# Expert units take their token rows by gathers from a normalized copy in DRAM instead of one-hot products

## The chip, the cores and the metric

The kernel runs on one core of a Trainium2 chip. The metric is the device time of one execution in microseconds (us). TensorE (PE) does the matmuls, VectorE (DVE), ScalarE (ACT) and GpSimd (POOL) the rest; SyncE (SP), ACT and POOL start transfers between DRAM and the on-chip memory, which 16 DMA engines carry out.

## The reference

512 tokens of width 1024 pass two layers of a first block and one of a second block. The change lies in the last stage, a mixture of experts with 32 experts in 4 groups, of which every token uses two:

```python
def hierarchical_moe(xn, w_group, b_group, w_expert, b_expert, w_gate, w_up, w_down):
    ...
    top_val, top_idx = lax.top_k(e_in, EXPERT_TOP_K)
    weights = p_group[:, None] * jax.nn.softmax(top_val, axis=-1)
    ...
    def run_block(args):
        tok, wt, e = args
        xb = xt[tok]
        hmid = jax.nn.silu(xb @ w_gate[e]) * (xb @ w_up[e])
        return (hmid @ w_down[e]) * wt[:, None].astype(xb.dtype)
    ...
# h = h + hierarchical_moe(rms_norm_2(h, g_ffn), ...), then rms_norm_2(h, g_final)
```

`xt` are the 512 normalized rows, `xb` those of the tokens that chose expert `e`. Everything is float32.

## The kernel before

Nearly all of the program before the experts is the same in both kernels. Each tile of 128 tokens keeps its rows in `h[t]` on the chip. As a tile gets ready, `moe_logits` (L1118) turns its rows, multiplies them with the gate weights and works out `r`, the factor that normalizes each row (`rstd`); `rn` keeps it. `moe_route` finds each token's two experts and the rank of each pick in its expert. `moe_first` (L1213) makes the tables of the first four blocks, `moe_plan` (L1229) those of all the others (`key`, `si`), on VectorE.

The picks of an expert fill blocks of 64 slots. A *unit* is one block with one expert's weights. There are 35 units: 32 first blocks, and at the units 8, 15 and 22 a second block of the same expert (here 8b, 15b, 22b), which uses weights that are already there. The first four units (`EARLY`) have fixed experts; which expert the others work for comes from `moe_plan`, and SP loads its number into a register before it starts their weights.

Each expert's weights are three pieces of 2 MiB: two for the way up (`gu`), one for the way down (`y`). They come by SP's queue into nine slots, so three experts' worth is on the chip; a piece for unit p+3 is started when the piece of unit p in its slot has been used for the last time, and SP starts the pieces one after the other, so that one that must wait holds up those behind it.

The loop in `moe` (L1459) writes, for unit u: `upwards` (the products `gu` with two of the pieces, then tanh on ACT and two products on DVE, tile `th`), `taken(u + 1)` (the next unit's rows), `down` (the products `y` of unit u-1, a copy, and a scatter of its rows to `picked` in DRAM by POOL), `hidden` (two transposes of `th`, tile `hT`), `turned` (four transposes of the next unit's rows `xg`, scaled by DVE into `xT`). The build may move instructions of different steps past each other where the data allow it.

`taken` (L1364) makes, on DVE, a one-hot matrix from the keys (tiles `kb`, `o`, `oh`), scaled with `rn`, multiplies it with all 512 rows on the tensor engine, and copies the result to `xg` on ACT:

```python
        for t in range(NT):
            for h in range(2):
                self.mm(pt[64 * h : 64 * h + 64, :], oh[:, t, :], self.h[t][:, 512 * h : 512 * h + 512],
                        start=t == 0, stop=t == NT - 1, tile_position=(0, 64 * h))
        nc.scalar.copy(xg, pt)
```

The products of one expert's work and these share the line L123 or L113 of the helpers `tr` and `mm`; in the profile they are told apart by tiles: `tr<-h,oh` are the one-hot products, `tr<-kf,xg` and `tr<-kf,th` the transposes, `gu<-we,xT` and `y<-we,hT` the expert's products. L1359 starts the weights, L1434 the scatters. After the loop the last unit's rows are weighed on the chip, `finish` (L1520) reads the scattered rows back, adds them, normalizes and writes the result.

Of the kernel before, what the change touches and what calls it, by code (L numbers as in the profile page):

```python
# [11 lines left out]
F32 = mybir.dt.float32  # L12
I32 = mybir.dt.int32
U32 = mybir.dt.uint32
AF = mybir.ActivationFunctionType
ALU = mybir.AluOpType
AX = mybir.AxisListType
PSUM = bass.MemoryType.PSUM
DRAM = bass.MemoryType.DRAM

P = 128
D = 1024
S = 512
# [3 lines left out]
EARLY = 4  # units whose experts are fixed  # L27
SECOND = (8, 15, 22)  # units whose experts may have a second block
NB = 32 + len(SECOND) + 16  # blocks of picks
HALF = (1, 0) * 32  # which of a token's weighted rows the tensor engine sums  # L30
# [36 lines left out]
class Beside:  # L67
    """A stage of n steps that runs beside others, from start to end on their scale."""
# [22 lines left out]
class K:  # L91
    """State that the stages of the kernel share."""
# [22 lines left out]
    # issue inst only once other is done, so that the group inst belongs to stays together  # L115
# [9 lines left out]
    # ---------------------------------------------------------------- set-up  # L125
# [34 lines left out]
    # (scale * x + eps) ** -0.5 for a narrow x: first guess from the bits, then Newton steps  # L160
# [19 lines left out]
    # dst[:, k, :] = transpose(h * rstd) * gs (+ sh), gs and sh per channel  # L180
# [14 lines left out]
    def psum_phase(self, **psbufs):  # L195
        """The PSUM rings of the phase that starts here."""
        es = ExitStack()
        self.ps = self.pool("ps", space=PSUM, es=es, reuse_waits="tile")
        self.psbufs = psbufs
        return es  # L200
# [5 lines left out]
    # where the experts' rows go, by picks; rows are read before the last have come  # L206
    def picked_open(self):
        self.yd = self.nc.dram_tensor("picked", [2 * S + NB, D], F32, kind="Internal").ap()
        self.yv = dram_disjoint_views(self.yd, 4)  # no two blocks scatter to the same row
        z = self.gp.tile([P, 2 * D], F32, tag="g", name="g")  # L210
        self.nc.gpsimd.memset(z, 0.0)
        for n in range(4):
            self.nc.gpsimd.dma_start(self.yd[n * 256 : n * 256 + 256, :].rearrange("(p r) d -> p (r d)", r=2), z)
# [9 lines left out]
    # ------------------------------------------------------- adaLN vectors  # L223
# [16 lines left out]
    # vector j (of 14, 1024 wide) of silu(c) @ [ada_w[0] | ada_w[1] | kv_ada_w] + bias: the products of  # L240
    # each partition are summed on the vector engine, or each of four groups of columns of the tensor
    # engine sums those of a fourth of the chunks; the sum over the partitions follows
# [52 lines left out]
    # g * (1 + scale) per channel  # L295
# [10 lines left out]
    # a row that comes by itself into t, early; later it is spread over the partitions by a product with ones  # L306
# [11 lines left out]
    # ------------------------------------------------------------- HGRN2  # L318
# [25 lines left out]
    # Within a tile of 128 tokens the decays are taken relative to the bounds of blocks of 16, 32, 64  # L344
    # and 128, so that no exponent but that of the 16-token blocks' own keys is positive.
    def hgrn(self, tiles, gs, sh, bufs, whole=False):
# [26 lines left out]
        for hd in range(8):  # L373
# [48 lines left out]
            # keys and queries relative to the bounds inside the tile  # L422
# [23 lines left out]
            # and relative to the tile's bounds  # L446
# [79 lines left out]
    # -------------------------------------------------------------- PEER  # L526
# [32 lines left out]
    # what goes into the PEER layer, by rows  # L559
# [8 lines left out]
    # expert numbers and gates of the tiles' 64 picks per token; alone: of each tile by itself  # L568
# [52 lines left out]
    # expert numbers and gates of a head's 16 picks, from the scores of its two halves  # L621
    def pick(self, sc):
# [39 lines left out]
        # exp(x) = ((1 + tanh(x / 4)) / (1 - tanh(x / 4))) ** 2: tanh lies in one table with gelu  # L662
# [62 lines left out]
    # ---------------------------------------------- stick-breaking mixer  # L725
# [4 lines left out]
    def sb(self, tiles, gk, shk, gq, shq):  # L730
# [50 lines left out]
        lo = [max(n - t0, 0) * P for n in range(nk)]  # first query column that key block n serves  # L781
        at = [(n % 2) * 256 for n in range(nk)]  # where block n lies in its bank
# [57 lines left out]
    # ------------------------------------- second block up to its experts  # L840
# [25 lines left out]
    # room for these tiles; early: their gates are worked out beside the attention  # L866
# [39 lines left out]
    # the first block's last norm  # L906
# [6 lines left out]
    # convolution and attention of some of the tiles  # L913
    def b2_first(self, tiles):
# [61 lines left out]
        # weights that are still there are used first  # L976
# [81 lines left out]
    # what follows on them, for all the tiles  # L1058
# [26 lines left out]
    # the way out  # L1085
# [13 lines left out]
    # ------------------------------------------------------------ experts  # L1099
    def moe_setup(self):  # L1100
# [8 lines left out]
        self.si0 = mp.tile([P, EARLY], I32, name="si0")  # L1109
        self.perm = mp.tile([P, 32], I32, name="perm")  # L1110
# [6 lines left out]
    # logits of tile t (of a pair), from its rows and what normalizes them  # L1117
    def moe_logits(self, t, space):  # L1118
# [15 lines left out]
        nc.vector.tensor_copy(self.rn[:, t : t + 1], r)  # L1134
        nc.vector.scalar_tensor_tensor(self.lg[:, t % 2, :], pl[:, :36], r, self.bge, op0=ALU.mult, op1=ALU.add)

    # experts, weights and ranks of the picks of tiles t and t + 1
    def moe_route(self, t):
# [47 lines left out]
        # weights: group probability times softmax over the two  # L1186
# [9 lines left out]
    # rows to gather (two halves of each token's row) and rows to scatter to for n blocks of 64 slots, from the  # L1196
    # slots and the blocks (one-hot) of the picks
    def moe_table(self, tag, n, slot, blocks, si):
# [10 lines left out]
        # an empty block's first slot takes a row that is there, and leaves one that no one reads  # L1209
        V.tensor_tensor(out=si, in0=f, in1=self.caps[:, :n], op=ALU.min)  # L1210

    # the tables of the first units' blocks, which need no more than the ranks
# [11 lines left out]
    # Experts are numbered from the last one down. Each one's picks fill blocks of 64 slots. Unit p works  # L1224
    # off the first block of one expert: of expert p, but that the first experts from EARLY on with more
    # than 64 picks change places with others, so that they lie at the units SECOND; their second blocks
    # follow there. Whatever else there is goes to further blocks, of which at most 16 are filled.
    # For each pick: its block and slot; for each block: the rows to scatter to.
    def moe_plan(self):  # L1229
# [26 lines left out]
        # least e whose prefix sum exceeds j, for j = 0 .. n - 1  # L1256
# [23 lines left out]
        # which expert each unit works for, and where each expert lies  # L1280
# [3 lines left out]
        for j, p in enumerate(SECOND):  # L1284
# [6 lines left out]
            # without such an expert, qe is zero and nothing moves  # L1291
# [12 lines left out]
        # block and slot of each pick  # L1304
# [30 lines left out]
        self.moe_table("y", NB, slot, av, self.si)  # L1335
        em = locate(ing, 16, "lm")
# [8 lines left out]
    def moe_open2(self):  # L1345
# [4 lines left out]
        self.xg = [self.mx.tile([P, 512], F32, name=f"xg{j}") for j in range(2)]  # L1350
        self.ng = 0

    # the weights of unit n, of expert e, by pieces: two that go up, and one that goes down
# [8 lines left out]
    # The rows of a block's tokens, those whose key in blocks lies from block on: a product of all  # L1362
    # rows with a one-hot matrix takes them.
# [19 lines left out]

    def space(self):
        self.ng += 1
        return self.xg[self.ng % 2]
# [12 lines left out]
    # Both halves of the tensor engine's columns work at a time: first each on half of the hidden  # L1399
    # units, then each on half of the outputs, for the same 64 tokens.  # L1400
# [38 lines left out]
    # where in a block a token's row goes, by weight: for either half of the outputs, slots by tokens  # L1439
# [19 lines left out]
    def moe(self):  # L1459
# [3 lines left out]
        units = []  # weights and block  # L1463
# [5 lines left out]
        def taken(u):  # L1469
            b = units[u][1]  # L1470
            return self.taken(self.key0, 64.0 * b) if b < EARLY else self.taken(self.key, float(b))
# [5 lines left out]
        x = self.turned(taken(0))  # L1477
        self.moe_plan()
        late = []
        last = len(units) - 1  # L1480
        for u, (p, b) in enumerate(units):
# [5 lines left out]
            x = taken(u + 1)  # L1487
# [3 lines left out]
            x = self.turned(x)  # L1491
            late.append((p, b, hT))
        down()
        # the last unit's rows are added on the chip
# [6 lines left out]
        # blocks that are left: then all over again, with all rows from DRAM  # L1501
# [13 lines left out]
    # an expert's number, for the engine that loads its weights  # L1515
# [3 lines left out]
    # the rows of the picks, by weight, from DRAM and from y, and the last norm  # L1519
# [41 lines left out]
    # ------------------------------------------------------------- program  # L1561
# [137 lines left out]
FIN = (0, 1, 1, 1)  # how many of a tile's two rows the tensor engine weighs at the end  # L1699
# [18 lines left out]
def prep(i):  # L1718
    """The inputs laid out for the kernel."""
# [3 lines left out]
    def kmaj(w, n):  # [K, N] -> [N / n, 128, K / 128, n]  # L1723
        k, m = w.shape
        return lay(w.reshape(k // P, P, m // n, n).transpose(2, 1, 0, 3))
# [13 lines left out]
    q, f, v, g = (w[:, o : o + 1024].reshape(8, P, 8, P) for o in (0, 1024, 2048, 3072))  # k p h n  # L1739
# [55 lines left out]
```

## Time and profile before

| | |
|---|---|
| times of three runs | 2838.49, 2839.49, 2849.84 us; median 2839.49 us |
| the profiled execution, first to last instruction | 2837.1 us (its own whole time is not given; the median lies 2.4 us above its span) |
| busy: PE, DVE, ACT, POOL | 86%, 69%, 28%, 26% of the span |
| DMA over the whole span | 342 GB/s |
| the loop over units | from about 2260 us to 2797 us of the span, then the last unit and the end |

Busy shares are means over stages that have different limits. What a change in the loop over units can be worth is read in that loop.

### The profile page before, as it was taken

To read this page: it belongs to the slowest core of one execution; us is meant where nothing else is said; L and a number is where in the kernel's file an instruction comes from. 1 tells how busy PE (TensorE), PEld (TensorE's weight loads), DVE (VectorE), ACT (ScalarE), POOL (GpSimd) and SP (SyncE) were. 2 spreads that over 40 slices of the span, in tenths; PEclk is the share of its full clock that TensorE was granted. 3 is DMA by queue.
4 is the path that set the end of the run, shared out by engine and by line. 5 is a ranking of instruction groups with operands and counts; after the bars stand their busy time and mean duration, and the time that the engine had idled before them with its cause. 6 is when DMAs were issued, how large, how long until landed. Compare 5 with 4: busy or idle time off the path is not lost.

```text
span 2837.1 us, 31101 instructions
## 1 busy us (share of the span) xinstructions
PE 2446.9 (86%) x10210; PEld 1491.1 (53%) x10210; DVE 1967.1 (69%) x5490; ACT 808.2 (28%) x1918; POOL 731.2 (26%) x576
## 2 busy tenths in 40 slices
PE   5999888878798787599887769689999999999997
PEld 3786456645466454166564435256888633333332
DVE  3886899997996689965577999878777532222224
ACT  2542255562221812122661121333113000000001
POOL 0000233333334344443343435423420000000000
PEclk9999989998999798799999879799999999999999
DMA  9875889999899799899889979888998679889794
GB/s 406 324 271 195 315 328 366 385 355 380 339 400 416 288 394 373 325 405 374 315 327 371 368 290 369 329 322 310 412 384 312 234 310 412 322 347 400 310 416 179
DMA packets 121556, 970.22 MB, mean 342 GB/s; under 512 B 15268, under 2 KB 16676, under 8 KB 20528
## 3 DMA queue, kind: packets, MB, share of 16 engines
q0 software_dynamic: 79904, 587.06, 53.3%
q1 hardware_dynamic: 39280, 375.51, 32.9%
q10 hardware_dynamic: 2208, 5.63, 0.6%
q8 instruction: 82, 1.34, 0.2%
q14 instruction: 82, 0.67, 0.1%
HBM read 955.71 MB, written 17.33 MB: 343 GB/s over the span
## 4 chain that ended last, share of the span: by engine, by line
PE 51%; DVE 27%; DMA 9%; issue 6%; ACT 6%; POOL 1%; ACTq 0%; POOLq 0%; SPq 0%; DVEq 0%
PE pj L113 16%; PE gu L113 9%; DVE g L697 8%; PE acc L113 7%; DMA g<-in_uv_dram,ex 6%; PE y L113 5%; PE tr L113 4%; PE rt L113 4%; PE mm L113 4%; DVE acc L716 4%; DVE y L947 3%; PE ad L113 2%; POOL g L694 1%; DMA w<-in_hgw_dram 1%; PE tr L123 1%
## 5 line engine op out<-in xcount | busy, mean ns | idle before, releaser
L694 POOL DMA_INDIRECT g<-in_uv_dram,ex x512 | 682.4, 1333 | 1173.8 <-DVE acc L716 431.9
L113 PE MATMUL acc<-g,dg 128*128 128x512 f32 x1056 | 595.0, 697 | 194.2 <-ACT dg L708 193.8
L697 DVE SCALAR_TENSOR_TENSOR g<-g,hn 128x1024 f32<-128x1024 f32 x512 | 621.4, 1218 | 102.1 <-DMA g<-in_uv_dram,ex 98.3
L113 PEld LDWEIGHTS acc<-g,dg 128*128 128x128 f32 x1056 | 215.6, 217 | 445.3 <-ACT dg L708 264.0
L716 DVE SCALAR_TENSOR_TENSOR acc<-g,wt,acc 128x1024 f32<-128x1024 f32 x240 | 306.7, 1278 | 3.5
L113 PE MATMUL gu<-we,xT 128*64 128x512 f32 x1120 | 256.6, 593 | 0.8 <-DVE xT L1394 0.8
L113 PE MATMUL pj<-hT,w 128*128 128x256 f32 (+1 forms) x1136 | 215.6, 344 | 4.4 <-DMA w<-in_win_dram 2.9
L1434 POOL DMA_INDIRECT picked<-y,si x34 | 33.2, 977 | 676.6 <-DVE y L1430 459.4
L113 PEld LDWEIGHTS pj<-hT,w 128*128 128x128 f32 x1136 | 185.6, 193 | 39.5 <-issue 16.5
L113 PE MATMUL pj<-hTa,w 128*128 128x256 f32 x768 | 180.9, 381 | 0.9 <-DVE sg L408 0.9
L113 PE MATMUL pj<-w,hT 128*128 128x256 f32 (+1 forms) x832 | 177.7, 371 | 0.0
L701 ACT ACTIVATE wt<-hid 128x2 f32<-128x2 f32 x256 | 51.8, 203 | 424.6 <-DVE g L697 423.3
L113 PEld LDWEIGHTS pj<-w,hT 128*128 128x128 f32 x832 | 152.7, 190 | 26.7 <-issue 8.1
L113 PEld LDWEIGHTS gu<-we,xT 128*64 128x64 f32 x1120 | 81.9, 137 | 159.6 <-issue 145.9
L1413 DVE SCALAR_TENSOR_TENSOR th<-th,gu 128x256 f32<-128x256 f32 x35 | 14.7, 421 | 214.9 <-ACT th L1412 214.9
L113 PEld LDWEIGHTS pj<-hTa,w 128*128 128x128 f32 x768 | 141.0, 191 | 24.4 <-issue 5.6
L113 PE MATMUL tr<-h,oh 128*64 128x512 f32 x560 | 152.7, 602 | 0.0
L113 PE MATMUL y<-we,hT 128*64 128x512 f32 x560 | 148.8, 593 | 0.2
L113 PE MATMUL rt<-hn2T,w 128*128 128x256 f32 (+1 forms) x640 | 123.7, 341 | 1.8 <-ACT hn2T L585 1.8
L708 ACT ACTIVATE dg<-kf,wt 128x128 f32<-128x128 f32 x264 | 101.5, 397 | 80.8 <-DVE wt L702 72.6
L947 DVE SCALAR_TENSOR_TENSOR y<-vb,wdw,y 128x128 f32<-128x128 f32 (+1 forms) x360 | 121.2, 389 | 1.4 <-ACT y L943 0.6
L113 PEld LDWEIGHTS rt<-hn2T,w 128*128 128x128 f32 x640 | 102.3, 193 | 23.0 <-issue 11.2
(476 smaller groups left out, 3366.0 us busy)
## 6 DMA issues: line engine op xcount, KB each, us to landing
we<-in_we_dram SPq DMA_DIRECT2D x96, 2048.0 KB
aw<-in_adaw_dram POOLq DMA_DIRECT2D x20, 2048.0 KB, 9.4
w<-in_win_dram SPq DMA_DIRECT2D x34, 1024.0 KB
w<-in_hgw_dram SPq DMA_DIRECT2D x32, 1024.0 KB
w<-in_pwq_dram SPq DMA_DIRECT2D x16, 1024.0 KB
w<-in_kvw_dram SPq DMA_DIRECT2D x16, 1024.0 KB
aw<-in_adaw_dram SPq DMA_DIRECT2D x4, 2048.0 KB
w<-in_hgwo_dram SPq DMA_DIRECT2D x8, 1024.0 KB
```

The source lines that it names most:

```text
L113: return self.nc.tensor.matmul(out, lhsT, rhs, start=start, stop=stop, **kw)
L123: return self.nc.tensor.transpose(out, in_, self.ident[:n, :n])
L694: nc.gpsimd.indirect_dma_start(out=g, out_offset=None, in_=uv, in_offset=bass.IndirectOffsetOnAxis(ap=picks[r // 16][0][:, r % 16 : r % 16 ...
L697: nc.vector.scalar_tensor_tensor(g[:, 0:D], g[:, 0:D], 1.0, hn, op0=ALU.mult, op1=ALU.mult, accum_out=hid[:, r : r + 1])
L701: nc.scalar.activation(wt[:, bs], hid[:, bs], AF.Gelu)
L708: nc.scalar.activation(dg, self.ident, AF.Copy, scale=wr)
L716: nc.vector.scalar_tensor_tensor(acc, g[:, D:], wr, acc, op0=ALU.mult, op1=ALU.add)
L947: nc.vector.scalar_tensor_tensor(y[:, c, :], vb[:, c, j : j + T], self.wdw[:, c, j : j + 1], y[:, c, :], op0=ALU.mult, op1=ALU.add)
L1413: nc.vector.scalar_tensor_tensor(th, th, 1.0, pg[:, :256], op0=ALU.add, op1=ALU.mult)
L1434: self.nc.gpsimd.indirect_dma_start(out=yv.rearrange("v (h d) -> (v h) d", h=2), out_offset=bass.IndirectOffsetOnAxis(ap=si, axis=0), in_= ...
```

## The change

For every unit from the fifth on (u = 4 to 34) the one-hot product goes. `moe_logits` now also writes the normalized rows of its tile to a DRAM tensor `xd` (one more pass of ACT over the tile and one transfer of 512 KB from ACT's queue). `moe_plan` works out a table `gi` of the rows to gather (four more small operations on DVE). `gathered` starts an indirect transfer on POOL's queue that fetches up to 128 half rows of 2 KB, those of one block, into `xg`. There are three `xg` now, and the loop asks for the rows of unit u+2 while it works on unit u. The first four units keep the one-hot products. The diff also takes out all comments; that is not shown.

```diff
 def moe_setup:
+        self.gi = mp.tile([P, NB], I32, name="gi")
+        self.xd = self.dp.tile([S, D], F32, name="xd")
 def moe_logits:
         nc.vector.tensor_copy(self.rn[:, t : t + 1], r)
+        xn = xT[:, 1].rearrange("p k n -> p (k n)")
+        nc.scalar.activation(xn, self.h[t], AF.Copy, scale=r)
+        nc.scalar.dma_start(self.xd[t * P : (t + 1) * P, :], xn)
 def moe_plan:
         self.moe_table("y", NB, slot, av, self.si)
+        odd = ts(tl(NB, "vi", I32), self.si, 1, None, ALU.bitwise_and)
+        ts(self.gi, self.si, 2, 1, ALU.logical_shift_right, ALU.logical_shift_left)
+        tt(self.gi, self.gi, odd, ALU.add)
+        ts(self.gi, self.gi, self.capg, None, ALU.min)
 def moe_open2:
-        self.xg = [self.mx.tile([P, 512], F32, name=f"xg{j}") for j in range(2)]
+        self.xg = [self.mx.tile([P, 512], F32, name=f"xg{j}") for j in range(3)]
+    def gathered(self, b):
+        xg = self.space()
+        self.nc.gpsimd.indirect_dma_start(
+            out=xg, out_offset=None, in_=self.xd.rearrange("s (h d) -> (s h) d", h=2),
+            in_offset=bass.IndirectOffsetOnAxis(ap=self.gi[:, b : b + 1], axis=0),
+            bounds_check=2 * S - 1, oob_is_err=False)
+        return xg
     def space(self):
         self.ng += 1
-        return self.xg[self.ng % 2]
+        return self.xg[self.ng % 3]
 def moe:
-        def taken(u):
-            b = units[u][1]
-            return self.taken(self.key0, 64.0 * b) if b < EARLY else self.taken(self.key, float(b))
+        rows = {}
+        def take(u):
+            if u <= last and u not in rows:
+                b = units[u][1]
+                rows[u] = self.taken(self.key0, 64.0 * b) if b < EARLY else self.gathered(b)
...
             th = self.upwards(p, x)
-            x = taken(u + 1)
+            take(u + 1)
+            if units[min(u + 2, last)][1] >= EARLY:
+                take(u + 2)
             if late:
                 down()
             hT = self.hidden(th)
-            x = self.turned(x)
+            x = self.turned(rows.pop(u + 1))
```

## Rows read from the trace of the kernel before

**Rows 1.** The page: span, and busy time of each engine (share) xinstructions.
```profile
span 2837.1 us, 31101 instructions
PE 2446.9 (86%) x10210; PEld 1491.1 (53%) x10210; DVE 1967.1 (69%) x5490; ACT 808.2 (28%) x1918; POOL 731.2 (26%) x576
```

**Rows 2.** Chain that ended last, 2399 to 2432 us: start, length, work.
```profile
2406.93 2.58 PE tr L113 x12
2410.36 3.43 PE y L113 x14
2413.79 0.81 PE tr L123 x6
2414.60 1.00 PE tr L113 x2
2415.60 6.87 PE gu L113 x31
```

**Rows 3.** Waits of PE, 2306 to 2797 us: total, times, longest.
```profile
PE tr L123 <- DVE th L1414: 16.9, 12, 1.5
```

**Rows 4.** Stretches: length, busy time by engine (xinstructions), granted clock, DMA share, GB/s.
```profile
2306.80:2783.00 476.20, 460.80 (x2127) 161.84 (x2124) 114.41 (x237) 42.02 (x94) 30.15 (x31) 1.00 0.90 369
2306.00:2417.50 111.50, 111.50 (x502) 37.05 (x502) 27.47 (x57) 9.46 (x21) 7.81 (x8) 1.00 0.98 401
2417.50:2430.00 12.50, 12.50 (x60) 4.24 (x56) 3.10 (x7) 1.17 (x3) 0.00 (x0) 1.00 0.01 5
2592.00:2652.00 60.00, 54.07 (x258) 19.63 (x257) 13.76 (x28) 4.82 (x11) 3.88 (x4) 1.00 1.01 427
2668.00:2682.00 14.00, 14.00 (x67) 4.74 (x64) 3.16 (x8) 1.35 (x3) 0.00 (x0) 1.00 0.06 18
2718.00:2768.00 50.00, 45.55 (x219) 16.62 (x217) 10.61 (x22) 4.05 (x9) 2.91 (x3) 1.00 1.01 428
2784.00:2797.00 13.00, 11.42 (x58) 4.04 (x56) 4.28 (x12) 0.77 (x2) 1.07 (x1) 1.00 0.03 12
```

**Rows 5.** Waits of SP's queue, 2399 to 2433 us: total, times, longest.
```profile
SPq L1359 <- PE tr L123: 22.2, 1, 22.2
```

**Rows 6.** DMA queues and issues, 2258 to 2837 us: packets, MB, share; KB each.
```profile
q1 hardware_dynamic: 13680, 188.75, 79.3%
q0 software_dynamic: 2720, 4.02, 1.9%
...
we<-in_we_dram SPq DMA_DIRECT2D x87, 2048.0 KB
```

**Rows 7.** Groups by line, 2306 to 2797 us: busy us, mean ns, idle before.
```profile
L113 PE MATMUL tr<-h,oh 128*64 128x512 f32 x496 | 133.7, 597 | 0.0
...
L1394 DVE TENSOR_TENSOR xT<-tr,cv 128x512 f32<-128x512 f32 x32 | 22.1, 692 | 14.0 <-PE tr L123 11.8
```

**Rows 8.** Chain that ended last, 2600 to 2617 us.
```profile
2602.23 3.58 PE tr L113 x16
```

**Rows 9.** One line's instructions (L1434, the scatters): ns min/median/max, landing.
```profile
L1434 POOL DMA_INDIRECT picked<-y,si x34: 966/971/1067, 2291.0 to 2798.1; - x34
...
DMA to landing us min/median/max: 2.5/8.1/10.2
```

**Rows 10.** Timeline of ACT and DVE ahead of the loop: start, length, instruction.
```profile
2238.24 1.06 ACT L176 ACTIVATE tmp<-h 128x1024 f32<-128x1024 f32 x1
...
2249.86 0.16 DVE L1369 TENSOR_SCALAR kb<-key 128x8 f32<-128x8 f32 x1
```

**Rows 11.** Chain that ended last, 2270 to 2840 us: units 3 and 31.
```profile
2306.80 6.87 PE gu L113 x31
...
2797.11 6.87 PE gu L113 x32
```

**Rows 12.** Stretches ahead of the loop, columns as in rows 4.
```profile
2241.80:2245.80 4.00, 1.31 (x6) 1.04 (x5) 3.79 (x33) 0.41 (x2) 0.00 (x0) 0.50 0.96 376
2245.80:2252.50 6.70, 6.69 (x30) 6.57 (x30) 4.56 (x21) 0.00 (x0) 0.00 (x0) 0.50 1.03 429
```

More of the change, by code (lines that the diff above doesn't have):

```diff
@@ L1475, in down @@
             self.scatter(self.downwards(n, hT), self.si0[:, b : b + 1] if b < EARLY else si[:, b : b + 1], self.yv[b % 4])
-        x = self.turned(taken(0))
+        last = len(units) - 1
+        take(0)
+        x = self.turned(rows.pop(0))
         self.moe_plan()
         late = []
-        last = len(units) - 1
         for u, (p, b) in enumerate(units):
```

## The prediction

> **What bounds the kernel now.** The page comes first: PE is busy for 86% of the span [rows 1]. That is a mean over stages, so the next view is the chain of waits inside the loop over units. There it runs over PE alone: one step, from the first `gu` of a unit to that of the next, is 15.54 us: 6.87 for `gu`, then the one-hot products, 3.43 and a little more for `y`, the transposes, and 1.00 in which two of the next unit's one-hot products stand between the transposes and the next `gu` [rows 2]. The waits of PE say the same: in 490 us it waits 16.9 us for `th` and for nothing else, never for weights [rows 3]. So at first sight whatever is taken from PE is gained.
>
> The stretches show what stands right behind PE. From the start of unit 3 to 2783 us, when the last weights have come, the DMA engines are busy for 0.90 of the time and move 369 GB/s [rows 4]. That mean hides two kinds of time. Over 111.5 us without a hole the share is 0.98, and at two later places 1.01. The rest is three holes of 12.5 to 14.0 us (two are shown) in which next to nothing moves [rows 4]. They lie at the second blocks, which need no weights: SP waits 22.2 us in one go for the slot that the late `y` of a unit frees [rows 5]. Outside the holes the weights are almost as slow as PE: a transfer-bound step lies just under a PE-bound one.
>
> **What the change removes from PE.** 31 units lose 16 one-hot products each; the group has 496 [rows 7]. Where they stand in one piece on the chain they take 3.58 us [rows 8]. Where the order is that of rows 2, two of them cover the time in which DVE makes `xT` (692 ns) [rows 7]; then up to 1.00 us [rows 2] comes back as idle time, if the build puts nothing else there. So a step loses between 2.58 and 3.58 us and becomes 12.0 to 13.0 us. For PE alone, 31 steps give 80 to 111 us: a span of 2726 to 2757 us. The removed work on DVE and ACT lies beside PE, so it counts for nothing.
>
> **What the weights allow.** The stretch from 2306.8 to 2783 us moved 369 GB/s x 476.2 us = 175.7 MB [rows 4]. The gathers add about what the scatters move, the same picks the other way: 4.02 MB for 34 of them [rows 6], so 3.7 MB for 31. Together 179.4 MB. The rate is the term that decides. Its lower bound is 401 GB/s (the first stretch, where SP starts pieces as PE frees them), its upper one 428 (two stretches) [rows 4]. With PE faster, the queue should always have weights left, which is the state of the 427 and 428 rows; small rows of 2 KB come between them. I take 420: 427 us, with 419 and 447 at the bounds. At 1.01 share there is no idle DMA left to use, so gathers are counted at their full bytes.
>
> The Trainium skill (DMA: Bandwidth & Descriptors, Specifications) gives a fabric ceiling of 435 GB/s. By it the same bytes are an estimated 412 us, and the end would be 15 us sooner than by the 427 us taken; no stretch here shows more than 428 GB/s.
>
> The holes should close. A hole needs PE to hold slots while the queue is empty. If weights are late, PE reaches a unit just as its first two pieces land, and then five or six pieces are still on their way or started: at 2.1 MB over 420 GB/s, 5.0 us each, 25 us or more. A second block takes PE 12 to 13 us, so the queue doesn't run dry.
>
> **The sum.** Transfers run from 2306.8 us, when unit 3 starts [rows 11]; until then the first four units are as before. The last piece lands at 2306.8 + 427.1 = 2733.9 us. The one before it, whose products are the second half of the last `gu`, lands 5.0 us earlier; half of 6.87 us [rows 11] follows, so `gu` ends at 2733.9 - 5.0 + 3.4 = 2732.3. From the end of that `gu` to the end of the span were 2837.1 - (2797.11 + 6.87) = 33.1 us [rows 1, 11]. They stay: `y` needs the last piece 1.6 us after that, when hidden units are only just being turned, and the scattered rows are read behind the weights instead of behind the last scatter. That gives 2765.4 us. PE alone could start its last `gu` 30 us before the weights let it, so the weights set the end.
>
> **What the change adds.** Per tile `moe_logits` gets an ACT pass of about 1.06 us [rows 10], which must wait for `r`, and behind it on ACT a transfer of 512 KB. The work queued behind it on ACT (copies and tanh of the stage beside it) is late by that much; for the first three tiles the products there cover it. For the last tile nothing covers it. The tile it reads from is released only when its transfer has landed; the next user of that room may be the first `kb` at 2249.86 us, 10.6 us after the pass over that tile which stands there now has ended [rows 10]; the rest of `rstd`, the new pass and the transfer must fit in between. Nothing to 5 us; I take 1. The four operations for `gi` are on tiles of 51 columns, beside PE, and the first gathered rows are turned only after unit 3 has begun: nothing. On POOL a gather is one instruction like the scatters, 0.97 us, with 15.5 us between them [rows 9]: nothing. Another 1 us goes for a slow clock in the last unit. Span 2767.4 us. The profiled span lies 2.4 us under the median, so the forecast is **2770 us**, 69 us or 2.4% faster.
>
> **The rivals.** A change of 0.5%, 14 us, is about what a measurement of this kernel can tell from none.
>
> *The weights bind* (the forecast): 2760 us at 428 GB/s without the small terms, to 2794 at 401 with 5 us ahead of the loop and 1 us in the last unit. Chance 0.70.
>
> *PE still binds, or the transfers are quicker.* 2728 to 2759 us, by PE's own sum. It would need 179.4 MB in under 419 us, more than any row shows, or part of the weights loaded before 2306.8. Chance 0.08.
>
> *The holes stay, or the gathers cost far more than their bytes.* If SP goes on waiting for a late `y` at each second block, the stream ends where it did, at 2783, plus 9 us of gathers: 2792 + 31.5 = 2823 us, 2826 as a time, and no measurable change. With one or two of them left it is 2783 to 2810. The in-order wait [rows 5] speaks for it; that PE would no longer be far enough behind the weights speaks against. Chance 0.12, a third of it within 0.5%.
>
> *The clock falls, and the kernel is slower.* PE would now wait for weights, about 3 us in each unit, where it waited 1.5 us at most before [rows 3]. Ahead of the loop PE worked for only 1.31 of 4.00 us, and the granted clock was 0.50 of full (1.2 GHz instead of 2.4) in that stretch and in the next one of 6.7 us, though PE was busy throughout it [rows 12]. That is 10.7 us at half speed, or 5.3 us of work lost. At each of 28 units with new weights it makes a step 12.5 + 5.3 = 17.8 us; with three at 12.5 the last `gu` starts at 2306.8 + 536 = 2843 instead of 2797, and the time is 2885 us. Up to some 3 us a unit such a loss hides in the wait for weights; slower than before it is from (490.3 - 31 x 12.5) / 28 = 3.7 us, where 490.3 us lie between the two starts of rows 11. Against it: a slower PE waits less for weights, so the fall feeds on itself only so far; and with waits of 1.5 us the clock stayed at 1.00 over 60 us [rows 3, 4]. Chance 0.07.
>
> The Trainium skill (TensorE: Matmul & The Clock Gate, HAM oscillation) says just this: waits for DMA between bursts of matmuls bring the slow clock back at each tile. Rows 12 agree for one fall; no run here shows it repeated in the loop.
>
> *The gathers land late.* A gather stands on POOL behind the scatter of unit u-2, so it starts about two steps, 24 us or more, before its rows are turned; the scatters land within 10.2 us, and 8.1 in the middle [rows 9]. It would make the kernel slower only if landing took about twice the old step, 31 us, where rows for two units are on their way. Then the step is that of the landing halved. Chance 0.03.
>
> **How the numbers follow.** The likeliest case gives 2770, with its own range 2760 to 2794. The whole range, **2748 to 2803**, takes in half of the quicker case and the cheaper half of the hole case, and leaves out some 0.2: the rest of these two and both slower ones. Faster by over 0.5%: 0.70 + 0.08 + 0.08 and a small part of the last two, 0.88. Within 0.5%: 0.05. Slower: 0.07.
>
> **What would show it.** Right: no `tr<-h,oh` after unit 3; the holes at the second blocks are gone, DMA share about 1.00 at 415 to 428 GB/s from 2307 to some 2734 us; PE now waits for `we` at most units, about 3 us each; steps of 15 us where weights are new and 12 to 13 for the rest; the last `gu` ends some 33 us before the end. Wrong: DMA share under 0.95 in that stretch with SP waiting on `y`; a granted clock of 0.5 for a large part of it; `tr<-kf,xg` waiting for the gathers; or a loop that begins over 5 us later than 2260.

## The result

| | median | runs | ratio to before (95% interval) |
|---|---|---|---|
| before | 2839.80 us | 2838.49 to 2849.84 | |
| changed | 2778.07 us | 2769.54 to 2783.62 | 0.9774 (0.9753 to 0.9794) |
| changed, measured once more beside `before` (then 2842.44 us) | 2768.73 us | 2768.31 to 2780.60 | 0.9756 (0.9733 to 0.9778) |

The forecast was 2770 us, between 2748 and 2803. The profiled execution of the changed kernel took 2769.54 us, its span is 2767.7 us; the sum gave 2767.4. The median is 61.7 us under that of the kernel before, where 69 was forecast. The profiled execution is the fastest of the four, and that it meets the sum to 0.3 us is luck, as the part on why shows.

The page of the changed kernel, for [rows 1], with the DMA share in 40 slices of the span:

```profile
span 2767.7 us, 30061 instructions
...
PE 2340.0 (85%) x9714; PEld 1481.2 (54%) x9714; DVE 1918.3 (69%) x5370; ACT 795.0 (29%) x1891; POOL 777.0 (28%) x607
...
DMA  9875889999989899999989889987999868999996
```

PE is as busy as before by share, and that says nothing. The view that does is the DMA line of the loop alone: its 510 us in 40 slices (the first row), with the issues of the gathers and scatters and their median time to landing.

```profile
DMA  6576999999999999999999999999999999998634
...
picked<-y,si POOLq DMA_INDIRECT x34, 8.4
xg<-xd,gi POOLq DMA_INDIRECT x31, 8.2
```

From the fifth slice to the last weights there is no hole: the three at the second blocks, two of them in [rows 4], are gone. In stretches, for [rows 4] and [rows 12] (columns as there):

```profile
2306.80:2700.00 393.20, 346.52 (x1589) 146.50 (x1585) 65.15 (x117) 22.23 (x58) 59.03 (x59) 0.99 1.01 424
2306.80:2736.40 429.60, 374.67 (x1715) 155.78 (x1711) 72.44 (x136) 25.06 (x66) 60.98 (x61) 0.99 0.99 417
2466.30:2469.80 3.50, 3.50 (x12) 1.06 (x10) 0.00 (x0) 0.00 (x0) 0.00 (x0) 0.51 1.00 421
```

In the first row the DMA engines are at 1.01 and 424 GB/s where they were at 0.90 and 369 on average; PE is idle for 47 of 393 us. The third row is one of the two places in the loop where the granted clock fell to 0.5.

The waits of PE, for [rows 3], from ahead of the loop to the end:

```profile
PE tr L123 <- DVE th L1434: 32.8, 22, 1.7
PE gu L113 <- DMA we<-in_we_dram: 18.5, 19, 2.0
```

The second row did not exist before: `gu` waits for weights at 19 places, 1.0 us on average. The first has about doubled from the 16.9 us of [rows 3]. The chain, for [rows 2], at the first fast units, at a later one, and where it leaves PE:

```profile
2317.07 6.87 PE gu L113 x32
2323.94 3.27 PE y L113 x14
2327.21 0.38 PE tr L123 x2
...
2327.67 0.39 ACT hT L1442
...
2328.11 1.07 PE y L113 x2
2329.18 6.87 PE gu L113 x32
...
2420.79 6.89 PE gu L113 x32
...
2427.71 0.39 ACT th L1432
...
2429.15 0.42 PE tr L123 x2
...
2430.09 3.65 PE y L113 x16
2433.74 6.89 PE gu L113 x32
...
2440.65 40.25 DMA we<-in_we_dram
```

```profile
2691.85 39.77 DMA we<-in_we_dram
2731.62 0.04 issue
2731.66 3.65 PE gu L113 x16
```

A step of PE is 12.11 us (2317.07 to 2329.18) as long as the weights loaded ahead last. The later one is 12.95 us (2420.79 to 2433.74), though it waits for no weights: the build has put all 16 products `y` behind the transposes, so nothing covers the work of ACT and DVE on `th`, and PE waits for it. From 2440 us on, the chain jumps back 33 to 41 us along the weights, five times, with steps of PE in between. It ends as the sum had it: the last two pieces, the second half of `gu`, then 32.4 us to the end (2767.7 - 2735.31; 33.1 was forecast).

### The profile page after: what moved, and what is told of

Read it like the earlier page. It is cut to its first block, busy times and chain, and to the rows that moved or that the text cites. A ratio compares the mean times of both kernels' runs of the same rounds, so it can differ in the third digit from the quotient of the medians.

```text
span 2767.7 us, 30061 instructions
## 1 busy us (share of the span) xinstructions
PE 2340.0 (85%) x9714; PEld 1481.2 (54%) x9714; DVE 1918.3 (69%) x5370; ACT 795.0 (29%) x1891; POOL 777.0 (28%) x607
## 4 chain that ended last, share of the span: by engine, by line
PE 43%; DVE 28%; DMA 16%; issue 6%; ACT 6%; POOL 1%; ACTq 0%; SPq 0%; POOLq 0%; DVEq 0%
PE pj L113 16%; DVE g L697 8%; DMA we<-in_we_dram 7%; DMA g<-in_uv_dram,ex 7%; PE acc L113 6%; PE gu L113 6%; PE mm L113 4%; DVE acc L716 4%; PE rt L113 3%; PE y L113 3%; DVE y L947 3%; PE ad L113 2%; POOL g L694 1%; DMA w<-in_hgw_dram 1%; PE mm L123 1%
## 5 line engine op out<-in xcount | busy, mean ns | idle before, releaser
L694 POOL DMA_INDIRECT g<-in_uv_dram,ex x512 | 695.3, 1358 | 1157.9 <-DVE acc L716 439.6
L113 PE MATMUL acc<-g,dg 128*128 128x512 f32 x1056 | 588.3, 690 | 191.4 <-ACT dg L708 191.0
L113 PE MATMUL gu<-we,xT 128*64 128x512 f32 x1120 | 258.9, 601 | 19.3 <-DMA we<-in_we_dram 18.5
L113 PEld LDWEIGHTS gu<-we,xT 128*64 128x64 f32 x1120 | 100.5, 138 | 166.3 <-issue 115.2
L113 PE MATMUL pj<-w,hT 128*128 128x256 f32 (+1 forms) x832 | 179.1, 373 | 0.0
L1398 POOL DMA_INDIRECT xg<-xd,gi x31 | 32.0, 1033 | 449.3 <-PE tr L123 233.1
L1432 ACT ACTIVATE th<-gu 128x256 f32<-128x256 f32 x35 | 13.4, 383 | 368.8 <-PE gu L113 368.8
```

The source lines that it names most:

```text
L113: return self.nc.tensor.matmul(out, lhsT, rhs, start=start, stop=stop, **kw)
L694: nc.gpsimd.indirect_dma_start(out=g, out_offset=None, in_=uv, in_offset=bass.IndirectOffsetOnAxis(ap=picks[r // 16][0][:, r % 16 : r % 16 ...
L1398: self.nc.gpsimd.indirect_dma_start(out=xg, out_offset=None, in_=self.xd.rearrange("s (h d) -> (s h) d", h=2), in_offset=bass.IndirectOffs ...
L1432: nc.scalar.activation(th, pg[:, :256], AF.Tanh, scale=0.5)
```

## The experiments

The theory, W in the expectations, is that of the forecast: after the change the stream of weights sets the end, and a gather costs what it takes out of that stream. The rivals are that PE still sets the end (P) and that the gathers do (G); others are named where they come up. The times carry a spread of some 10 us that has nothing to do with the change. It comes from ahead of the loop, as far as the first start of `gu` in single profiled executions shows. Rows of the tile `gu` (instructions, ns, first and last start): the kernel before, the changed kernel twice, then the run with gathers one unit ahead (below):

```profile
L113 PE MATMUL gu<-we,xT x1120: 592/592/644, 2259.9 to 2803.4; 128*64 128x512 f32 x187
```

```profile
L113 PE MATMUL gu<-we,xT x1120: 592/592/1061, 2257.9 to 2734.7; 128*64 128x512 f32 x187
```

```profile
L113 PE MATMUL gu<-we,xT x1120: 592/592/1057, 2257.5 to 2733.9; 128*64 128x512 f32 x187
```

```profile
L113 PE MATMUL gu<-we,xT x1120: 592/592/644, 2264.3 to 2740.6; 128*64 128x512 f32 x187
```

The last three have spans of 2767.7, 2766.9 and 2773.7 us; from that start to the end it is 509.8, 509.4 and 509.4 us. This length, called *the loop* below, is the sharper measure, though it comes from one profiled execution of each kernel; for the kernel before it is 2837.1 - 2259.9 = 577.2 us.

| run | median us | ratio (95% interval) | loop us |
|---|---|---|---|
| before | 2839.80 | | 577.2 |
| changed | 2778.07 | 0.9774 (0.9753 to 0.9794) | 509.8 |
| no gathers | 2766.07 | 0.9724 (0.9700 to 0.9748) | 496.6 |
| gathers and products | 2842.09 | 0.9997 (0.9983 to 1.0011) | 577.4 |
| changed, two thirds of the weights | 2732.05 | 0.9611 (0.9585 to 0.9638) | 465.0 |
| one unit ahead | 2774.08 | 0.9754 (0.9726 to 0.9781) | 509.4 |
| before, two thirds of the weights | 2837.19 | 0.9983 (0.9969 to 0.9998) | 571.4 |
| products for every second unit | 2794.08 | 0.9826 (0.9802 to 0.9850) | 530.1 |
| gathers from unit 1 | 2770.97 | 0.9744 (0.9716 to 0.9771) | 505.1 |
| gathers doubled, other tile | 2828.54 | 0.9951 (0.9937 to 0.9965) | 568.6 |
| gathers doubled, same tile | 2788.34 | 0.9810 (0.9783 to 0.9837) | 522.9 |
| products for every fourth unit | 2774.08 | 0.9762 (0.9740 to 0.9784) | 509.0 |
| gathers from unit 2 | 2770.72 | 0.9753 (0.9734 to 0.9771) | 507.0 |

**No gathers.**

```diff
 def gathered(self, b):
         xg = self.space()
-        self.nc.gpsimd.indirect_dma_start(out=xg, ...)
         return xg
```

> The changed kernel without the gathers: units from the fifth on work on whatever rows are already in their buffer, so the expert rows are not those of their tokens; everything else is done. Theory W (the stream of weights sets the end, and a gather costs its bytes in that stream): 3.7 to 4.0 MB less at 425 GB/s, so 9 us less than the changed kernel, about 2769 us against its 2778. Theory P (PE still sets the end): no change, 2778 us. Theory G (the landing of the gathers sets the pace): 30 us less or more.

The loop is 13.2 us shorter (12.0 by the medians): W, with a dearer gather than its bytes. PE waits for `th` as before (32.9 us), and its waits for weights fall from 18.5 to 8.9 us. PE alone setting the end (P) is out, and so are gathers that set the pace (G).

**Gathers and products.**

```diff
                 rows[u] = ... else self.gathered(b)
+                if b >= EARLY:
+                    self.taken(self.key, float(b), self.scr[:, :512])
...
```

> The changed kernel with the gathers, and with the one-hot products of the units from the fifth on made as well, into a buffer that nobody reads: nothing is left out. Theory W: PE is the bound again at a step of 15.5 us, the holes in the stream of weights come back, and the gathers cost nothing beside it: 2835 to 2845 us, the time of the kernel before. Theory P: the same. Theory G: the gathers were dear and the products cheap: under 2800 us, or over 2855 if gathers and products add up.

2842.09 us, the time before. The DMA share in 40 slices of 2258 to 2768 us shows the holes again:

```profile
DMA  4565799999999199999999729999999962999999
```

So the products, and not where rows come from, are what the change takes off the bound; and where PE binds, 31 gathers and the copy in DRAM cost nothing measurable.

**Two thirds of the weights, after and before.** Only one diff; the same lines went into the kernel before.

```diff
 def expert_weights:
+            if j == 2 and n >= 3:
+                self.ws[n, 2] = self.ws[n - 3, 2]
+                continue
```

> The changed kernel without loading the weights for the way down from unit 3 on: those of units 0 to 2 are used again, so outputs of the experts are not the reference's; 61 MB of the weights are not moved. Theory W: the stream no longer binds, PE does, with steps of 12.0 to 13.0 us: 2728 to 2759 us. Theories P and G: no change from the changed kernel, about 2778 us.

> The kernel before, without loading the weights for the way down from unit 3 on (those of units 0 to 2 are used again, so outputs of the experts are not the reference's). Theory W (before, the one-hot products kept PE the bound): no change, 2835 to 2845 us. Theory C (before, weights and PE bound together, and either could be eased): faster by over 0.5%, under 2825 us.

The stretch of the changed kernel with these lines, and of the kernel before with them:

```profile
2309.40:2680.00 370.60, 367.64 (x1657) 209.51 (x1656) 66.70 (x120) 23.11 (x61) 61.00 (x60) 1.00 0.81 315
```

```profile
2307.50:2790.00 482.50, 482.40 (x2175) 160.87 (x2176) 117.49 (x246) 42.89 (x96) 31.18 (x32) 1.00 0.60 234
```

In both PE is busy from end to end. Taking a third of the weights away is worth 46 us after the change (2778.07 - 2732.05) and next to nothing before: ratio 0.9983, 5 us. So before, the weights lay just under PE and hardly bound (C is out); after, they do. In the order of these runs PE alone would allow 2732 us; from unit 3 on every step of the first is 12.11 us but the last, and PE doesn't wait for `th` in either. The order in the changed kernel is another, with 32.8 us of such waits; why the build makes it so stays open.

**One unit ahead.**

```diff
             take(u + 1)
-            if units[min(u + 2, last)][1] >= EARLY:
-                take(u + 2)
```

> The changed kernel asking for the rows of unit u+1 instead of u+2 while it works on unit u; nothing is left out. Theory W: a gather is then started about one step, 12 us, before its rows are turned and lands in 8 to 10 us, and PE has 2 to 3 us of waiting to give away: no change, 2773 to 2785 us. Theory G: the rows come late at each unit: over 2800 us.

No difference, in the loop within 0.4 us. The second unit of lead is not needed here.

**Products for every second and every fourth unit.**

```diff
-  rows[u] = ... else self.gathered(b)
+  rows[u] = ... else self.taken(self.key, float(b)) if u % 2 else self.gathered(b)
```

> The changed kernel with the one-hot products put back for every second unit from the fifth on, and gathers for the others; nothing is left out. Theory W: two steps of PE take 15.5 + 12.1 us, 13.8 on average, still less than the 15 us of the weights, and half of the gathers' bytes are gone: 2765 to 2780 us, no slower than the changed kernel. Theory P (PE sets the end, each product costs its 3.5 us): halfway back, about 2810 us.

This missed: 16 us slower than the changed kernel, not level with it. The stretch, and PE's waits for `th` (2300 to 2790 us), tell why:

```profile
2306.80:2750.00 443.20, 416.25 (x1934) 158.67 (x1934) 93.33 (x187) 33.92 (x81) 47.17 (x47) 1.00 0.97 403
```

```profile
PE tr L123 <- DVE th L1434: 25.3, 17, 1.5
```

DMA is at 0.97, and PE waits for no weights in this run, only for `th`: PE binds again. The expectation had set PE's mean over all steps against the 15 us of a unit that loads weights. But three of the 31 steps load none; the weights allow 429.6 / 31 = 13.9 us a step. And PE's mean is not 13.8: from the first `gu` of unit 3 (2308.95 us) to that of the last unit (2751.13) it is 14.3 us, since the waits for `th` come on top of steps of 12.11 and 15.54. With `u % 4 == 1` in place of `u % 2`:

> The changed kernel with the one-hot products put back for every fourth unit from the fifth on; nothing is left out. Theory W with its sum put right (28 of 31 steps need weights, so the weights allow 13.9 us a step and PE, at 12.1, has 1.8 us to give): one product in four adds 0.9 us or so to PE's mean step, which stays under 13.9: no slower than the changed kernel, 2770 to 2781 us. Theory P: 8 to 9 products of 3.5 us, 2806 us.

2774.08 us; the loop is 509.0 against 509.8 us. Eight products put back cost nothing, fifteen cost 16 us (20 in the loop). The sum in this expectation is still too generous, as it has PE at 12.1 us: with eight products PE waits for no weights any more, but for `th` as long as before (2300 to 2760 us):

```profile
PE tr L123 <- DVE th L1434: 31.7, 21, 1.7
```

What PE has to give is nearer to 31 us, an estimate from the fifteen: 15 x 3.43 us less the 20 that they cost. That is 1.0 us a step.

**Gathers doubled.** First into a tile that nobody reads, then twice into the same rows.

```diff
-        self.nc.gpsimd.indirect_dma_start(out=xg, ...)
+        for x in (self.scr[:, :512], xg):     # first run; second run: (xg, xg)
+            self.nc.gpsimd.indirect_dma_start(out=x, ...)
```

> The changed kernel with every gather done twice, the first of the two into a tile that nobody reads; nothing is left out. Theory W with the price of the gathers as the run without them gave it (12 us for 31): 12 us more than the changed kernel, about 2790 us. Theory B (a gather costs only its bytes at the rate of the weights): 9 us more. Theory N (gathers cost nothing; the run without them was faster by chance): no change.

50 us instead of 12 (59 in the loop). Waits of POOL and of PE from 2300 to 2480 us, and stretches of this run:

```profile
POOL scr L1399 <- DMA scr<-xd,gi: 134.4, 27, 13.0
```

```profile
PE tr L123 <- DMA xg<-xd,gi: 26.8, 3, 17.0
```

```profile
2334.00:2480.00 146.00, 86.00 (x334) 31.82 (x334) 13.27 (x25) 4.61 (x12) 39.34 (x40) 0.75 0.70 272
2480.00:2800.00 320.00, 277.48 (x1284) 108.67 (x1280) 54.06 (x102) 18.99 (x50) 46.95 (x47) 0.99 0.99 418
```

The idle gathers all write one tile, so each waits for the one before it, and the build put many of them ahead of gathers that are needed: POOL waits for landings 27 times, and units wait up to 17.0 us for their rows. The run prices POOL's order, not the gathers. Hence the second form:

> The changed kernel with every gather done twice into the same rows, so that the second waits for the first and POOL's order is kept; nothing is left out. Theory W with the price from the run without gathers: 12 us more than the changed kernel, about 2790 us. Theory L (the earlier doubled run was slow because gathers wait for each other on POOL's queue, not for the bytes): if a gather now still lands before its rows are turned, 2785 to 2795 us and no wait of PE for gathers; if it doesn't, such waits show and it is over 2800.

2788.34 us; the loop is 522.9 us, 13.1 above the changed kernel, about as much as it was below without gathers. PE doesn't wait for gathers:

```profile
PE tr L123 <- DVE th L1435: 32.8, 22, 1.7
PE gu L113 <- DMA we<-in_we_dram: 27.6, 20, 2.9
```

Queue q0 (scatters and gathers; packets, MB, share of the 16 engines) from 2306 to 2736 us, without gathers, with them, doubled:

```profile
q0 software_dynamic: 2695, 3.99, 2.5%
```

```profile
q0 software_dynamic: 4960, 7.80, 4.9%
```

```profile
q0 software_dynamic: 7207, 11.39, 7.1%
```

Each set of gathers moves 3.6 to 3.8 MB in 2.2 to 2.4% of 430 us, 10 us of all engines; the other 3 us of the 13.2 are not accounted for.

**Gathers for early units.** A table made in `moe_first`, in `gi[:, :EARLY]`; products only for unit 0, later only for units 0 and 1.

```diff
-  rows[u] = self.taken(self.key0, 64.0 * b) if b < EARLY else self.gathered(b)
+  rows[u] = self.taken(self.key0, 64.0 * b) if b < 1 else self.gathered(b)   # second run: b < 2
...
```

> The changed kernel with gathers also for units 1 to 3, by a table that is made ahead of the plan; only unit 0 keeps the one-hot product, nothing is left out. Theory W: three steps of 15.5 us become 12.1, slots come free up to 10 us earlier, and the idle time of the stream of weights between units 0 and 4 (some 12 us) shrinks by as much: 6 to 10 us less than the changed kernel. Theory S (the stream is paced by its own rate from the start of the loop): no change.

> The changed kernel with gathers also for units 2 and 3, by a table that is made ahead of the plan; units 0 and 1 keep the one-hot products, nothing is left out. Theory W: two steps of 15.5 us become 12.1, and without the wait for the first gather that the run with gathers from unit 1 had: 5 to 7 us less than the changed kernel in the same call. Theory S (the stream is paced by its own rate from the start of the loop): no change.

Neither differs measurably from the changed kernel (2770.97 and 2770.72 against 2778.07 and 2768.73); the loop is 4.7 and 2.8 us shorter, under the 6 to 10 and the 5 to 7 that were expected. The idle time of the stream that should have shrunk stayed. A stretch of the changed kernel, then one of the run with gathers from unit 2:

```profile
2273.00:2288.00 15.00, 15.00 (x72) 6.55 (x72) 5.36 (x18) 1.11 (x3) 1.09 (x1) 1.00 0.41 151
```

```profile
2275.00:2288.00 13.00, 12.96 (x59) 4.54 (x59) 5.06 (x16) 0.77 (x2) 1.58 (x2) 1.00 0.15 38
```

In the second, SP waits once for 18.6 us for a `y` (waits of SP's queue, 2260 to 2300 us):

```profile
SPq L1376 <- PE y L113: 18.6, 1, 18.6
```

In the changed kernel SP waits there for `gu` and `tr` alone. PE is faster in the second run, but what SP's pieces wait for changed with it, and one piece that needs a `y` holds up those behind it. Another order of the pieces was not tried.

**The changed kernel once more**, beside the last variants.

> The changed kernel itself, once more, beside the other runs of this call: 2770 to 2784 us, as before.

The median is 2768.73 us (2768.31 to 2780.60), a microsecond under the range expected, and the loop is the same within 0.4 us.

## Why the prediction was right

*What bounds before.* PE, with the weights just under it: shown from both sides, by the products made beside the gathers (2842 us) and by a third of the weights taken away (5 us; 5.8 in the loop).

*What PE loses.* Forecast 80 to 111 us; with a third of the weights gone from both kernels the loop is 571.4 - 465.0 = 106.4 us shorter, 3.43 a step. It is near the upper end, because the 1.00 us that was to come back as idle time is filled: the build puts two of the `y` products there (1.07 us in the chain above), so a step is 12.11 us.

*What the weights give back.* 44.8 us after the change (509.8 - 465.0), where they cost 5.8 before, so 67 us are left (106.4 + 5.8 - 44.8). The sum had 179.4 MB at 420 GB/s in 427.1 us; the same stretch moved 417 GB/s x 429.6 us = 179.1 MB. For most of it the rate was 424, near the upper of the two bounds; over the last pieces it falls.

*The gathers.* The mis-sized term: 3.7 MB at the stream's rate is 9 us, measured are 13.2, or 0.43 us for each of 31. The excess shows in the rate: from unit 3 to the last weights it is 421 GB/s without gathers, 417 with them and 413 with twice as many, where the sum took 420 for all bytes. From the start of unit 3, now at 2304.6 us, to the last piece at 2736.4 it is 431.8 us, 4.7 over the 427.1 of the sum.

*The luck.* That excess is made good by terms beside it: unit 3 starts 2.2 us earlier than the sum had it, the 1 us ahead of the loop and the 1 us for a slow clock in the last unit are not seen, and the end takes 32.4 us where 33.1 was forecast.

*What PE waits for.* This part of the picture was wrong. Forecast were waits for weights of about 3 us at most units, and steps of 15 us where weights are new. In the trace these waits are 18.5 us in all, and 32.8 us go to `th`, which the sum didn't have. So not all of the 44.8 us is PE waiting for weights. That the stream of transfers still sets the end rests on its share of 1.01 over 393 us, in which there is no room left, and on the loop that follows the gathers by 13 us either way while the waits for `th` stay (32.9 and 32.8 us). No run has all the weights with the order of PE in which it doesn't wait for `th`.

*The holes.* All three closed, as forecast.

*Ahead of the loop.* The forecast had 1 us, 5 at most. No delay is seen: first `gu` at 2257.9 and 2257.5 us against 2259.9 before. Experiments whose code ahead of the loop is that of the changed kernel began it as late as 2269.7 us (without gathers), so the spread of this stage is larger than the term, and larger than the 5 us that were to show the forecast wrong.

*The clock.* It was a rival at 0.07. PE waits 1.0 us at a time for weights, 2.0 at most, and the clock fell twice in the loop, for some 3.5 us each, where the rival had 10.7 us at each unit. The same kernel once more shows one such fall and the run with gathers one unit ahead none, and the loop is the same within 0.4 us: here the loss hides in the wait for weights. The rule of the Trainium skill that was set beside it (TensorE: Matmul & The Clock Gate, HAM oscillation) holds where waits are long: in the run with idle gathers PE was busy for 86 of 146 us, and the granted clock was 0.75 over that stretch. The short waits that this change leaves didn't bring the slow clock back at each unit.

*Late gathers.* Not in this order on POOL; one unit of lead is enough. The first doubled run shows the mechanism of that rival at work, with a wait of POOL's own making in place of a slow landing.

## What to carry to other kernels

Before work is taken off the bounding engine, add up what the next one needs over the same stretch, holes counted as room: here PE had 106 us to give up and 67 came out, which one view by stretches (DMA share, GB/s, holes) foretold to a few us. Take such a mean over all steps, those that load nothing too, and count what the engine waits for in its own order; the slack was about 1 us a step, not 3. Beyond that point a saving on PE buys nothing: with or without the last eight products the loop is the same within 1 us. And the small gathers beside a full stream were paid in full, and more.

## What the runs showed that was not expected

A gather of some 60 rows of 2 KB costs 0.43 us of a saturated weight stream, in both directions (without: -13.2 us, doubled: +13.1 us), half as much again as its bytes. And indirect transfers that have to wait for one another on POOL's queue cost far more than that: 50 us for 31 that nobody needed.
